# Turning the gated product in 32x32 blocks and through DRAM in place of TensorE transposes

## The chip, the cores and the metric

One core of a Trainium2 chip runs the whole program. The metric is the device time of one execution in microseconds, taken as the median of several runs.

## What is computed

Two transformer-like blocks follow each other on 256 rows of 1024 values in float32. The first has four feed-forward networks (FFNs) of width 2816 around a convolution module and a latent attention; the second has two, with a mixer between them and with modulation vectors that a product of a condition vector with a large matrix gives. An FFN is what the change touches:

```python
def swiglu_ffn(h, w1, w3, w2):
    return (jax.nn.silu(h @ w1) * (h @ w3)) @ w2

def first_block(...):
    for i in range(DEPTH):
        h = h + FFN_RES_WEIGHT * swiglu_ffn(rmsnorm(h, ffn_norm1[i]), ffn1_w1[i], ffn1_w3[i], ffn1_w2[i])
        m = rmsnorm(h, mix_norm[i])
        ...
        h = h + FFN_RES_WEIGHT * swiglu_ffn(rmsnorm(h, ffn_norm2[i]), ffn2_w1[i], ffn2_w3[i], ffn2_w2[i])

# second block, around the mixer, with shift, scale and gate from mod = silu(c) @ w_mod + b_mod
x = x + 0.5 * g1 * swiglu(modulate(rmsnorm_2(x, norm_ffn1), sh1, sc1), w_ffn1_in, w_ffn1_out)
...
x = x + 0.5 * g3 * swiglu(modulate(rmsnorm_2(x, norm_ffn2), sh3, sc3), w_ffn2_in, w_ffn2_out)
```

## The kernel before

Each float32 operand is split into a high part in fp32r and the rest, also in fp32r; `mm3` (L108) makes a product of three matrix products (high by high, high by low, low by high). `split` (L82, L83) has ScalarE write the high part and VectorE the low one. Weights come in units of 1 MB (128 rows of 2048 values): SP loads one into one of four `raw` buffers (L63), and `piece` splits it in four parts of 512 columns into `whi` and `wlo`. Of these there are 16 for W1 and W3, two steps' worth, and 8 for W2, two steps' worth as well.

The 256 rows are two row tiles, t = 0 and 1. An FFN goes through its width in eleven steps j of 256 columns (`NF = 11`). In a step, `load(j)` brings two units of W1 and W3 and one of W2; `gu(j, t)` makes the 24 products of `cols` (h with W1 beside W3, into a PSUM bank with the tag `wk`) and the gate: ScalarE writes the silu `sg` (L340), VectorE the gated product `gg` (L342), 128 rows by 256. For the product with W2 it must lie the other way round, so `turn(j, t)` has TensorE transpose it in two blocks of 128x128 against a unit matrix (L106), into a `wk` bank, and splits the result into `gh` and `gl`. `down(j, t)` makes 12 products of it with W2 and adds them up in the two `acc` banks of its row tile. Of a normal step the program has gu(j, 0), gu(j, 1), then down(j - 1, 0), turn(j, 0), down(j - 1, 1), turn(j, 1). The last step does gu(10, 0), down(9, 0), turn(10, 0) and half of cols(10, 1) before down(10, 0), so that row tile 0 is done early.

A planner orders the instructions of each engine ahead of time by what it thinks is ready, in the order of the program where several are. While `self.pinned` is set, TensorE's instructions keep the program's order (L99 to L106). In the FFNs that is so for steps 0 and 1 only. Each engine then works through its list in order, and an instruction that waits holds back those behind it. SP issues all transfers before the change.

In f0 to f4 a step with an even j, from 2 on, also makes a group of modulation values (`mid`, `mod_group`): four steps in f0, f1 and f2, three in f3 and f4, 18 in all. It loads two units, sums them with VectorE in `macc` (L987, L991), splits the sum, makes two products, loads a row of bias into `mrow` (L1001), adds it (L1002) and stores the row to DRAM (L1015). f5 has none.

In the convolution, the kernel already takes data through DRAM: `ship` (L570, L577) writes 128 partitions of 2 runs of 636 bytes and reads them back in four transfers of 32 partitions of 8 runs of 624 bytes, on SP's queue.

Of the kernel before, what the change touches and what calls it, by code (L numbers as in the profile page):

```python
# [10 lines left out]
F32 = mybir.dt.float32  # L11
F32R = mybir.dt.float32r
# [7 lines left out]
P = 128  # L20
# [11 lines left out]
class Build:  # L32
# [284 lines left out]

    def ffn(self, w, finish, after, mid=None, slow=False, begun=None):
        nc, tc = self.nc, self.tc
        with tc.tile_pool(name=f"ffn{self.n}", bufs=1) as fp:  # L320
            self.fp = fp
            acc = [[self.bank(tag="acc") for _ in range(2)] for _ in range(2)]
            g, w2 = {}, {}

            u = {}

            def up(j):
                u[j] = [self.unit(w[3 * j + i]) for i in range(2)]

            def down_in(j):  # L330
                w2[j] = self.unit(w[3 * j + 2], pool=fp)

            def load(j):
                up(j)
                down_in(j)

            def gate(j, t, ps):
                sc = 1.0 if self.rs[t] is None else self.rs[t][:, :1]
                sg = self.t([P, 256], tag="sg", bufs=2, pool=fp)
                nc.scalar.activation(sg, ps[:, :256], AF.Silu, scale=sc)  # L340
                g[j, t] = self.t([P, 256], tag="gg", bufs=3, pool=fp)
                nc.vector.scalar_tensor_tensor(  # L342
                    out=g[j, t], in0=ps[:, 256:], scalar=sc, in1=sg, op0=ALU.mult, op1=ALU.mult
                )

            def gu(j, t):
                gate(j, t, self.cols(t, u[j], 512))

            def turn(j, t):
                hi = self.t([P, 2, P], F32R, tag=f"gh{t}", bufs=2, pool=fp)  # L350
                lo = self.t([P, 2, P], F32R, tag=f"gl{t}", bufs=2, pool=fp)
                self.transposed(g[j, t], 2, hi, lo)
                g[j, t] = hi, lo

            def down(j, t):
                self.rows(acc[t], g[j, t], w2[j], j == 0, j == NF - 1)

            if begun:
                u[0] = begun[0]
                for t in range(2):  # L360
                    gate(0, t, begun[1][t])
                with self.in_turn():
                    up(1)
                turn(0, 0)
                gu(1, 0)
                down_in(0)
                turn(0, 1)
                gu(1, 1)
                turn(1, 0)
                down_in(1)  # L370
            else:
                load(0)
                load(1)
                gu(0, 0)
                gu(1, 0)
                self.flush()
                turn(0, 0)
                gu(0, 1)
                turn(1, 0)
                gu(1, 1)  # L380
                turn(0, 1)
            down(0, 0)
            turn(1, 1)
            down(0, 1)
            self.pinned = False
            for j in range(2, NF - 1):
                load(j)
                gu(j, 0)
                gu(j, 1)
                if mid:  # L390
                    mid(j)
                for t in range(2):
                    down(j - 1, t)
                    turn(j, t)
            j = NF - 1
            load(j)
            gu(j, 0)
            down(j - 1, 0)
            turn(j, 0)
            ps = self.cols(1, u[j], 512, ks=range(4))  # L400
            down(j, 0)
            finish(0, acc[0])
            post = after(0)
            gate(j, 1, self.cols(1, u[j], 512, ps, range(4, 8)))
            down(j - 1, 1)
            turn(j, 1)
            if not slow:
                post()
            down(j, 1)
            finish(1, acc[1])  # L410
            self.pending.append(after(1))
            if slow:
                post()

    def out_rows(self, x, units, finish, after, mid=None):


        acc, done, post = {}, [0, 0], []

        def step(order):  # L420
            for c in order:
                if c in "pm":
                    (post[0] if c == "p" else mid)()
                    continue
                t = int(c)
                if t not in acc:
                    acc[t] = [self.bank(tag="acc") for _ in range(2)]
                i = done[t]
                z = tuple(v[:, 2 * i : 2 * i + 2] for v in x[t])
                self.rows(acc[t], z, units[i], i == 0, i == 3)  # L430
                done[t] += 1
                if i == 3:
                    finish(t, acc[t])
                    (self.pending if t else post).append(after(t))

        return step
# [539 lines left out]
    def mod_group(self, i):  # L976

        nc, a = self.nc, self.a
        part, which, cols = i // 6, i % 6 // 2, slice(i % 2 * 512, i % 2 * 512 + 512)
        acc = self.t([P, 512], tag="macc", pool=self.fp)  # L980
        for u in range(2):
            r = self.raw(a["wmod"][2 * i + u])
            for k in range(4):
                w = r[:, k * 512 : k * 512 + 512]
                s = self.cact[:, 4 * u + k : 4 * u + k + 1]
                if u == k == 0:
                    nc.vector.tensor_scalar(  # L987
                        out=acc, in0=w, scalar1=s, scalar2=None, op0=ALU.mult
                    )
                else:  # L990
                    nc.vector.scalar_tensor_tensor(  # L991
                        out=acc, in0=w, scalar=s, in1=acc, op0=ALU.mult, op1=ALU.add
                    )
        hi = self.t([P, 512], F32R, tag="mhi", pool=self.fp)
        lo = self.t([P, 512], F32R, tag="mlo", pool=self.fp)
        self.split(hi, lo, acc)
        ps = self.bank()
        self.matmul(ps, self.onesr, hi, start=True, stop=False)
        self.matmul(ps, self.onesr, lo, start=False, stop=True)
        row = self.t([1, 512], tag="mrow", pool=self.fp)  # L1000
        nc.sync.dma_start(out=row, in_=a["b_mod_2"][0:1, i * 512 : i * 512 + 512])  # L1001
        nc.vector.tensor_add(row, ps[:1, :], row)  # L1002
        if which == 1:
            name = ("norm_ffn1_2", "norm_mix_2", "norm_ffn2_2")[part]
            grow = self.t([P, 512], tag="junk")[:1]
            nc.sync.dma_start(out=grow, in_=a[name][0:1, cols])
            nc.vector.scalar_tensor_tensor(
                out=row, in0=row, scalar=1.0, in1=grow,
                op0=ALU.add, op1=ALU.mult,
            )  # L1010
        elif which == 2:
            nc.vector.tensor_scalar(
                out=row, in0=row, scalar1=0.5, scalar2=None, op0=ALU.mult
            )
        nc.sync.dma_start(out=self.mods[i], in_=row)  # L1015
# [553 lines left out]
```

## Time and profile before

| | us |
|---|---|
| median of 3 runs | 1547.34 |
| lowest, highest | 1544.97, 1547.45 |
| the profiled execution's own time | 1546.88 |
| its span in the profile | 1545.1 |
| TensorE busy | 1517.2 |
| VectorE busy | 1093.9 |
| ScalarE busy | 831.2 |
| GpSimd busy | 36.0 |

The span reaches from the first to the last recorded instruction, and the profiled execution's own time is 1.8 us longer. An engine is busy while one of its instructions runs; matrix products overlap, so that TensorE's busy time is no measure of its speed. The DMA engines' share is that of the 16 engines' time in which packets were under way.

### The profile page before, as it was taken

Reading aid. Unit: us, or ns where it says so; the run is one execution under the profiler, and the core shown is the slowest. Engines: PE = TensorE matmul, PEld = TensorE weight load, DVE = VectorE, ACT = ScalarE, POOL = GpSimd, SP = SyncE. Lnnn points to the kernel's source line nnn. Section 1 sums busy time; section 2 is a strip of 40 time slices with the busy share of each in tenths; the row PEclk is TensorE's granted clock in tenths of the full one; section 3 lists DMA queues with packets and bytes.
Section 4 is the critical chain, followed back from the end, with each engine's and each line's share of the span. In section 5 each row is a group of like instructions: output and inputs, shape, how many; then the busy total and the mean of one; then the engine's idle time right before and its main releaser. Section 6 shows DMA issues by size and latency. Waiting matters only on the chain.

```text
span 1545.1 us, 21226 instructions
## 1 busy us (share of the span) xinstructions
PE 1517.2 (98%) x7824; PEld 1240.3 (80%) x7824; DVE 1093.9 (71%) x2136; ACT 831.2 (54%) x1723; POOL 36.0 (2%) x52
## 2 busy tenths in 40 slices
PE   8999998999999999999999999999999999999998
PEld 6888887788888888888788888788887877888886
DVE  7977566487775877657579765788657886876552
ACT  7555463465554655446475554545545565665541
POOL 0000000000000000000000000100001100000000
PEclk9999999999999999999999999999999999999999
DMA  8886477377664576643358755387552443565530
GB/s 312 305 291 252 171 239 186 115 277 284 245 245 164 218 270 249 235 137 119 127 195 310 263 191 191 127 307 275 207 191 95 161 167 112 192 255 186 196 109 28
DMA packets 61580, 316.69 MB, mean 205 GB/s; under 512 B 9210, under 2 KB 19706, under 8 KB 25764
## 3 DMA queue, kind: packets, MB, share of 16 engines
q1 hardware_dynamic: 61476, 315.34, 57.4%
q8 instruction: 61, 1.00, 0.3%
q14 instruction: 43, 0.35, 0.1%
HBM read 312.93 MB, written 2.39 MB: 204 GB/s over the span
## 4 chain that ended last, share of the span: by engine, by line
PE 90%; DVE 4%; issue 2%; DMA 2%; ACT 1%; POOL 1%; SPq 0%; POOLq 0%; DVEq 0%; ACTq 0%
PE wk L103 51%; PE acc L103 35%; PE wk L106 4%; DVE wlo L83 1%; DMA raw<-in_pw_dram 1%; POOL sm L130 1%; DMA h<-in_x_dram 0%; DVE sm L1190 0%; DMA shift<-ut 0%; DVE y L259 0%; DVE h L1033 0%; DVE y L1032 0%; DMA shifted<-shift 0%; ACT pb L1202 0%; DVE pb L1243 0%
## 5 line engine op out<-in xcount | busy, mean ns | idle before, releaser
L83 DVE TENSOR_TENSOR wlo<-raw,whi 128x512 fp32r<-128x512 f32 x996 | 652.3, 684 | 62.9 <-ACT whi L82 60.8
L82 ACT CAST whi<-raw 128x512 fp32r<-128x512 f32 x996 | 587.7, 619 | 95.4 <-PE acc L103 24.3
L103 PE MATMUL wk<-whi,xh 128*128 128x512 f32 x1120 | 443.8, 396 | 0.5
L103 PE MATMUL wk<-whi,xl 128*128 128x512 f32 x1120 | 437.8, 391 | 0.0
L103 PE MATMUL wk<-wlo,xh 128*128 128x512 f32 x1120 | 437.7, 391 | 0.0
L103 PEld LDWEIGHTS wk<-whi,xl 128*128 128x128 f32 x1120 | 210.9, 188 | 45.0
L103 PEld LDWEIGHTS wk<-whi,xh 128*128 128x128 f32 x1120 | 211.1, 188 | 43.5 <-ACT xh L85 1.5
L103 PEld LDWEIGHTS wk<-wlo,xh 128*128 128x128 f32 x1120 | 211.1, 188 | 42.1
L103 PE MATMUL acc<-whi,gh 128*128 128x512 f32 x528 | 212.2, 402 | 0.9 <-ACT gh L82 0.9
L103 PE MATMUL acc<-whi,gl 128*128 128x512 f32 x528 | 207.3, 393 | 0.0
L103 PE MATMUL acc<-wlo,gh 128*128 128x512 f32 x528 | 206.7, 392 | 0.0
L340 ACT ACTIVATE sg<-wk,sm 128x256 f32<-128x256 f32 x88 | 41.7, 474 | 196.5 <-PE wk L103 195.1
L342 DVE SCALAR_TENSOR_TENSOR gg<-wk,sm,sg 128x256 f32<-128x256 f32 x88 | 42.3, 481 | 110.4 <-ACT sg L340 109.1
L103 PE MATMUL acc<-whi,xh 128*128 128x512 f32 (+2 forms) x304 | 117.9, 389 | 0.7 <-ACT xh L82 0.7
L103 PEld LDWEIGHTS acc<-whi,gl 128*128 128x128 f32 x528 | 99.1, 188 | 21.7
L103 PEld LDWEIGHTS acc<-whi,gh 128*128 128x128 f32 x528 | 99.3, 188 | 21.4 <-ACT gh L82 2.1
L103 PE MATMUL acc<-wlo,xh 128*128 128x512 f32 (+2 forms) x304 | 116.1, 382 | 0.0
L103 PE MATMUL acc<-whi,xl 128*128 128x512 f32 (+2 forms) x304 | 115.7, 382 | 0.0
L103 PEld LDWEIGHTS acc<-wlo,gh 128*128 128x128 f32 x528 | 99.4, 188 | 19.9
L82 ACT CAST gh<-wk 128x256 fp32r<-128x256 f32 x132 | 48.8, 370 | 121.4 <-PE wk L106 121.3
L83 DVE TENSOR_TENSOR gl<-wk,gh 128x256 fp32r<-128x256 f32 x132 | 55.4, 419 | 64.4 <-ACT gh L82 64.3
L991 DVE SCALAR_TENSOR_TENSOR macc<-raw,cact,macc 128x512 f32<-128x512 f32 x126 | 94.4, 749 | 2.8
(278 smaller groups left out, 1162.1 us busy)
## 6 DMA issues: line engine op xcount, KB each, us to landing
raw<-in_f_dram SPq DMA_DIRECT2D x196, 1024.0 KB
raw<-in_wmod_dram SPq DMA_DIRECT2D x36, 1024.0 KB
raw<-in_win_dram SPq DMA_DIRECT2D x16, 1024.0 KB
raw<-in_pw_dram SPq DMA_DIRECT2D x12, 1024.0 KB
shifted<-shift SPq DMA_DIRECT2D x32, 156.0 KB
raw<-in_wo_dram SPq DMA_DIRECT2D x4, 1024.0 KB
raw<-in_wbr_dram SPq DMA_DIRECT2D x4, 1024.0 KB
raw<-in_wout_dram SPq DMA_DIRECT2D x4, 1024.0 KB
```

The lines of the kernel that those rows point to most:

```text
L82: i = nc.scalar.copy(hi, src)
L83: j = nc.vector.tensor_tensor(out=lo, in0=src, in1=hi.bitcast(F32), op=ALU.subtract)
L103: return self.pin(self.nc.tensor.matmul(*args, **kw))
L106: return self.pin(self.nc.tensor.transpose(out, src, ident))
L130: self.nc.gpsimd.tensor_tensor(out=r, in0=v, in1=self.mhalf[:, :1].to_broadcast([P, w]), op=ALU.pow)
L340: nc.scalar.activation(sg, ps[:, :256], AF.Silu, scale=sc)
L342: nc.vector.scalar_tensor_tensor(out=g[j, t], in0=ps[:, 256:], scalar=sc, in1=sg, op0=ALU.mult, op1=ALU.mult)
L991: nc.vector.scalar_tensor_tensor(out=acc, in0=w, scalar=s, in1=acc, op0=ALU.mult, op1=ALU.add)
```

## The change

In steps 1 to 9 the gated product is turned without TensorE. VectorE transposes each block of 32x32 within its place (`blocks`), both row tiles into one tile `gb`. Four transfers that GpSimd issues (`move`), one for every 32 partitions, write the blocks to DRAM, each block's row of 32 values (128 bytes) to where it belongs, 512 such runs per transfer. One more (`back`) reads the turned product into `gt`, 128 partitions of four runs of 512 bytes, and ScalarE and VectorE split it from there. Each step has its own place in DRAM. Steps 0 and 10 keep the transposes on TensorE.

In the program's order, `move(j)` stands behind gu(j, 1) and `back(j)` behind down(j - 1, 1). The last step is now pinned to the program's order. Two things change to make room: `gg` has two buffers in place of three, and the row of bias is loaded into row 0 of `macc`, once that is split, and not into a tile of its own.

```diff
     def ffn(self, w, finish, after, mid=None, slow=False, begun=None):
         nc, tc = self.nc, self.tc
-        with tc.tile_pool(name=f"ffn{self.n}", bufs=1) as fp:
+        with ExitStack() as ctx:
+            name = f"ffn{self.n}"
+            fp = ctx.enter_context(tc.tile_pool(name=name, bufs=1))
+            dram = ctx.enter_context(
+                tc.tile_pool(name=name + "d", bufs=1, space=bass.MemoryType.DRAM)
+            )
...
-                g[j, t] = self.t([P, 256], tag="gg", bufs=3, pool=fp)
+                g[j, t] = self.t([P, 256], tag="gg", bufs=2, pool=fp)
...
+            def parts(t):
+                return tuple(
+                    self.t([P, 2, P], F32R, tag=f"{n}{t}", bufs=2, pool=fp) for n in ("gh", "gl")
+                )
+
             def turn(j, t):
-                hi = self.t([P, 2, P], F32R, tag=f"gh{t}", bufs=2, pool=fp)
-                lo = self.t([P, 2, P], F32R, tag=f"gl{t}", bufs=2, pool=fp)
-                self.transposed(g[j, t], 2, hi, lo)
-                g[j, t] = hi, lo
+                pair = parts(t)
+                self.transposed(g[j, t], 2, *pair)
+                g[j, t] = pair
+
+            turned = {}
+
+            def blocks(j, t):
+
+                if t == 0:
+                    turned[j] = self.t([P, 2, 256], tag="gb", pool=fp)
+                nc.vector.transpose(turned[j][:, t], g[j, t])
+
+            def move(j):
+
+                d = dram.tile([2, 2, P, P], F32, name=f"{name}_{j}")
+                to = d.rearrange("t k (c f) (a s) -> a f (t k c) s", f=32, s=32)
+                for a in range(4):
+                    nc.gpsimd.dma_start(
+                        out=to[a],
+                        in_=turned[j][32 * a : 32 * a + 32].rearrange("p t (b s) -> p (t b) s", s=32),
+                    )
+                turned[j] = d
+
+            def back(j):
+                r = self.t([P, 2, 2, P], tag="gt", pool=fp)
+                nc.gpsimd.dma_start(
+                    out=r.rearrange("p t k s -> p (t k) s"),
+                    in_=turned[j].rearrange("t k p s -> p (t k) s"),
+                )
+                for t in range(2):
+                    g[j, t] = parts(t)
+                    self.split(*g[j, t], r[:, t])
...
                 gu(1, 0)
+                blocks(1, 0)
                 down_in(0)
                 turn(0, 1)
                 gu(1, 1)
-                turn(1, 0)
+                blocks(1, 1)
                 down_in(1)
...
+            move(1)
             down(0, 0)
-            turn(1, 1)
             down(0, 1)
+            back(1)
             self.pinned = False
             for j in range(2, NF - 1):
                 load(j)
-                gu(j, 0)
-                gu(j, 1)
+                for t in range(2):
+                    gu(j, t)
+                    blocks(j, t)
+                move(j)
                 if mid:
                     mid(j)
                 for t in range(2):
                     down(j - 1, t)
-                    turn(j, t)
+                back(j)
+            self.pinned = True
             j = NF - 1
             load(j)
             gu(j, 0)
...
             if slow:
                 post()
+            self.pinned = False
...
-        row = self.t([1, 512], tag="mrow", pool=self.fp)
+        row = acc[:1]
```

## Rows read from the trace of the kernel before

**Rows 1.** The page's first part: busy us, share of the span and instructions
```profile
PE 1517.2 (98%) x7824; PEld 1240.3 (80%) x7824; DVE 1093.9 (71%) x2136; ACT 831.2 (54%) x1723; POOL 36.0 (2%) x52
```

**Rows 2.** The chain that ended last, shares by engine and by line
```profile
PE 90%; DVE 4%; issue 2%; DMA 2%; ACT 1%; POOL 1%; SPq 0%; POOLq 0%; DVEq 0%; ACTq 0%
PE wk L103 51%; PE acc L103 35%; PE wk L106 4%; DVE wlo L83 1%; DMA raw<-in_pw_dram 1%; POOL sm L130 1%; DMA h<-in_x_dram 0%; DVE sm L1190 0%; DMA shift<-ut 0%; DVE y L259 0%; DVE h L1033 0%; DVE y L1032 0%; DMA shifted<-shift 0%; ACT pb L1202 0%; DVE pb L1243 0%
```

**Rows 3.** Windows of one f5 step and of two f1 steps: engines' busy us
```profile
core 0: us, PE busy (x) PEld busy (x) DVE busy (x) ACT busy (x) POOL busy (x), PEclk, DMA share, GB/s
1382.07:1398.97 16.90, 16.90 (x77) 13.85 (x77) 9.54 (x17) 8.69 (x16) 0.00 (x0) 1.00 0.54 194
357.08:391.21 34.13, 34.13 (x156) 28.09 (x155) 26.45 (x45) 17.92 (x33) 0.00 (x0) 1.00 0.71 254
```

**Rows 4.** The chain in order of time, f0 and f5: start us, us, what
```profile
161.19 10.93 PE wk L103 x48
...
178.04 5.49 PE wk L103 x24
...
1409.89 2.77 PE acc L103 x12
1412.88 2.77 PE acc L103 x12
1415.87 10.92 PE wk L103 x48
```

**Rows 5.** TensorE's timeline, last step of f0: start us, us, instruction
```profile
183.36 0.39 PE L103 MATMUL acc<-whi,gh 128*128 128x512 f32 x1
```

**Rows 6.** Timeline of a step in f1 and one in f5
```profile
370.80 0.39 PE L103 MATMUL acc<-whi,gh 128*128 128x512 f32 x1
...
371.88 0.48 DVE L342 SCALAR_TENSOR_TENSOR gg<-wk,sm,sg 128x256 f32<-128x256 f32 x1
...
1392.83 0.40 PE L103 MATMUL acc<-whi,gh 128*128 128x512 f32 x1
...
1393.61 0.42 DVE L342 SCALAR_TENSOR_TENSOR gg<-wk,sg 128x256 f32<-128x256 f32 x1
...
1395.60 0.38 PE L106 MATMUL wk<-ident,gg 128*128 128x128 f32 x2
...
1396.02 0.37 ACT L82 CAST gh<-wk 128x256 fp32r<-128x256 f32 x1 [2.10 <-PE wk L106]
```

**Rows 7.** VectorE's groups by line and form: busy us, mean ns, idle before
```profile
L83 DVE TENSOR_TENSOR wlo<-raw,whi 128x512 fp32r<-128x512 f32 x980 | 645.7, 687 | 61.4 <-ACT whi L82 59.3 <-DMA raw<-in_f_dram 0.5
...
L83 DVE TENSOR_TENSOR gl<-wk,gh 128x256 fp32r<-128x256 f32 x132 | 55.4, 419 | 64.4 <-ACT gh L82 64.3
...
L987 DVE TENSOR_SCALAR macc<-raw,cact 128x512 f32<-128x512 f32 x18 | 8.7, 484 | 8.6 <-DMA raw<-in_wmod_dram 8.5
...
L1280 DVE TENSOR_SCALAR pb<-pb,sm 128x256 f32<-128x256 f32 x16 | 4.6, 349 | 0.1
```

**Rows 8.** The convolution's transfers on SP: issue ns min/median/max, first and last start
```profile
L577 SPq DMA_DIRECT2D shifted<-shift x32: 303/448/1233, 216.5 to 271.0; - x32
L570 SPq DMA_DIRECT2D shift<-ut x8: 360/377/397, 213.9 to 264.8; - x8
```

**Rows 9.** SP's timeline in the convolution: one write and its reads
```profile
213.89 0.38 SPq L570 DMA_DIRECT2D shift<-ut  x1
216.50 1.83 SPq L577 DMA_DIRECT2D shifted<-shift  x4
```

**Rows 10.** The chain in order of time: waits for the convolution's transfers
```profile
254.44 5.67 DMA shift<-ut
262.30 3.84 DMA shifted<-shift
```

**Rows 11.** DMA view of 217 to 220 us: packets, and the queue's share
```profile
DMA packets 957, 0.57 MB, mean 189 GB/s; under 512 B 48, under 2 KB 957, under 8 KB 957
...
q1 hardware_dynamic: 957, 0.57, 88.7%
```

**Rows 12.** What SP's queue waited for: us in total, times, longest us
```profile
SPq L63 <- DVE wlo L83: 770.1, 173, 21.1
```

More of the change, by code (lines that the diff above doesn't have):

```diff
@@ L375, in ffn @@
                 gu(1, 0)
+                blocks(1, 0)
                 self.flush()
@@ L378, in ffn @@
                 gu(0, 1)
-                turn(1, 0)
                 gu(1, 1)
+                blocks(1, 1)
                 turn(0, 1)
+            move(1)
             down(0, 0)
-            turn(1, 1)
             down(0, 1)
+            back(1)
             self.pinned = False
```

## The prediction

> **What bounds the kernel now.** I read the busy shares first. TensorE has work in 1517.2 of 1545.1 us; GpSimd has 52 instructions and is free [rows 1]. The chain that ended last says the same from its end: 90% is TensorE, 51% in the products with W1 and W3, 35% in the accumulation with W2, and 4% in the transposes by line 106 [rows 2]. So a shorter TensorE program is a shorter kernel wherever nothing else comes late. Two stretches show how much else there is: a step without a modulation group has VectorE busy 9.54 of 16.90 us and the transfers at 0.54 of the DMA engines' time; two steps with one group between them have 26.45 of 34.13 us and 0.71. TensorE is busy all the time in both [rows 3].
>
> The chain in order of time gives the step's parts. 48 products take 10.92 us, and 12 accumulations 2.77 us, but the next piece begins 1412.88 - 1409.89 = 2.99 us later: the two transposes of one turn stand between and take 0.22 us [rows 4]. They last 0.38 us by themselves, but overlap with their neighbours [rows 6].
>
> **What is removed.** The turns of steps 1 to 9, two row tiles each, in six FFNs: 108 turns of 0.22 us, 23.8 us of TensorE. All lie on the chain. The step becomes 16.90 - 0.44 = 16.46 us. Steps 0 and 10 keep theirs.
>
> **What is put in its place, and how long it takes.** The new path starts where cols(j, 1) ends and must be done when down(j, 0) begins. I add it up from that end:
> - Gate: in one step without a group the product is written at 1393.61 + 0.42 us, 1.20 us after the first accumulation started at 1392.83; in a step with one, 371.88 + 0.48 - 370.80 = 1.56 us [rows 6]. I take 1.4.
> - The transpose on VectorE isn't in the trace. Its shape, 128x256 in f32, costs 349 ns as a tensor-scalar and 419 ns with two operands [rows 7]: 0.35 to 0.42, and up to 0.69 more behind one weight piece. I take 0.5. The 108 of them add 45 us to VectorE; a pair of steps goes to about 28.1 of 33.2 us, which TensorE's own time covers. If that cover went, they would cost 0.4 us each.
> - Four transfers out of 512 runs of 128 bytes, then one back of 512 runs of 512 bytes, all issued by GpSimd. No row shows GpSimd issuing. Nearest is SP with 32 partitions of 8 runs: 0.30 us at the least, 0.45 in the median, 1.23 at the most [rows 8]. I keep 0.30 as the low end, and twice 1.23, for twice the runs, as the high one. Runs written out by a program are nearer the slow rows than the fast: I take 1.0 each, so 4.0 for the four.
> - Landing of the last of them: the convolution writes 159 KB and starts its read 216.50 - 213.89 - 0.38 = 2.2 us after issue [rows 9]; in a crowded place the wait was 5.67 us [rows 10]. I take 2.6, since weights are loaded beside it.
> - Issue of the transfer back 1.0, again 0.30 to 2.46. Its landing: 3.84 us where the convolution waited for its read [rows 10], 2.2 as in the write at best; I take 3.0.
> - The high part on ScalarE before the first accumulation: 0.37 us [rows 6], 0.6 with a hand-over.
>
> Sum: 1.4 + 0.5 + 4.0 + 2.6 + 1.0 + 3.0 + 0.6 = 13.1 us. All low ends give 7.8, all high ends about 25.6.
>
> The Trainium skill has a price of its own, in "DMA: Bandwidth & Descriptors", section "Anatomy of one DMA — SWDGE (gpsimd) path": some 2.0 us fixed for a GpSimd transfer plus its bytes at 436 GB/s, issue included, which would be an estimate of 2.15 us for the last one out and 2.6 us for the one back. No row here shows such a transfer. With it the path would be 1.4 + 0.5 + 3.0 + 2.15 + 2.6 + 0.6 = 10.3 us and the forecast that of the first rival below.
>
> **The time there is for it.** In a regular step, down(j - 1) and cols(j + 1) lie between: 5.54 + 10.92 = 16.46 us. 13.1 fits, with 3.4 to spare. At the last step it doesn't: step 10 does only cols(10, 0) before down(9, 0), and TensorE's order is now pinned there. In the first FFN cols(9) ends at 161.19 + 10.93 = 172.12 and the first accumulation of down(9, 0) starts at 183.36 [rows 4, 5]: 11.24 us, less two turns 10.8. So TensorE waits 13.1 - 10.8 = 2.3 us once in each FFN, 13.8 us in six. In f5, where nothing comes after, the same holds.
>
> **The other edits.** Two buffers for the product in place of three: the next write of a buffer is a step later, 16 us against a path that has read it after 2. The bias row now lies in row 0 of the modulation sum, so its load, on SP, waits until VectorE has split that sum, and the add on VectorE waits for the load. Behind it on SP stand the next weight loads, behind the add on VectorE the next weight pieces. A landing of 2.2 us, 18 times, is 40 us of delay in all; SP waits 770.1 us for VectorE to free weight buffers anyway [rows 12], and VectorE has some 5 us left in each pair of steps. I cost it at nothing; with that cover gone it is 40 us.
>
> The transfers add 2560 packets to a step. Where small ones ran alone, 957 packets took 88.7% of 16 engines for 3 us, 44 ns each [rows 11]; by bytes a 128-byte one would be 9 ns and a 512-byte one 36. A step gets 2.3 to 7.0 us of the DMA engines' time. The plain step goes from 9.1 to at most 16.1 of 16.46 us. The pair with a group goes from 24.2 to between 28.8 and 38.2 of 33.2: that can fail. I take the middle, 33.5, which just about fits, and cost it at nothing.
>
> **Sum.** 1546.88 us, the profiled execution's own time (span 1545.1 and 1.8 around it), less 23.8 plus 13.8, is 1536.9. The median of the three runs is 0.5 us above that execution, so 1537.
>
> **Rivals.**
> 1. All hidden: the path is under 10.8 us, as it is if an issue costs 0.5 us. Then 23.8 us are gained: 1523.5. For it, SP's median; against it, the runs per issue.
> 2. A little later than I think: between 14.25 and 15.3 us the six waits give back all but 3.1 us of the gain, or exceed it by no more: no change, 1544 to 1550.
> 3. Late in every step, the opposite sign. Place: the issue on GpSimd, one after another. At 1.9 us each the path is 17.6 us. Each FFN's last wait is 6.8 us, 41 in all; in the eight regular steps TensorE waits for 17.6 - 16.46 = 1.1 us at every second one (a wait gives the next path that much more room), 27 in all: 1546.9 - 23.8 + 41 + 27 = 1591. It decides from 15.3 us of path. The steps between aren't pinned, and the planner may put cols(j + 2, 0) ahead of down(j, 0) where it sees the lateness coming; that would take the 27 away, not the 41.
> 4. The transfers become the bound in the FFNs with groups: 38.2 against 33.2 us is 5 us a pair, 18 pairs, 90 us: 1627 with the forecast's own terms; at 35 ns a packet 2.2 a pair, 1577. For it: loads there already arrive at 0.71. Against: 44 ns is of packets of 624 bytes.
> 5. VectorE holds GpSimd's descriptor writing off. If GpSimd only got on in VectorE's gaps, its 5.0 us of issue would grow by 1 / (1 - 26.45 / 34.13) = 4.4 in a pair with a group: 22 us, a path of 30, some 13 late at every second step. With half of the 48 regular windows as such places, 24 x 13.6 + 6 x 19 less 23.8 is over 400 us; the time would be near 1960. Against it: the frequent pieces run at 687 ns for 512 elements with two operands, and only a form like the tensor-scalar of 484 ns, 18 in all, goes faster over the same 512 [rows 7]. The Trainium skill states this rule in "SBUF — State Buffer", section "Who interferes with whom", for VectorE's two-port modes; no run here shows it yet.
>
> **How the numbers follow.** Chances: the forecast (path 10.8 to 14.25, gain 3 to 24) 0.36; rival 1 0.11; rival 2 0.11; rival 3 0.25; rival 4 0.12; rival 5 0.05. A change under 0.2%, 3.1 us, can't be told from none here. So faster 0.47, same 0.11, slower 0.42. The predicted time is that of the forecast, whose own range is 1523 to 1544. The range of 8 in 10 reaches from 1520, just below rival 1, to 1612, where the path is 18.3 us: what is left out is the upper part of rivals 3 and 4, and rival 5.
>
> **What would show it.** Transposes of gg on line 106 fall from 264 to 48, and a step without waits is 16.46 us. Right: GpSimd's issues near 1.0 us, no wait of TensorE in the middle of an FFN, one of about 2 us before down(9, 0). Wrong: issues near 2 us with TensorE waiting for gh in the steps between (rival 3), a DMA share of 1.0 between weight loads and ScalarE waiting for raw (rival 4), issues that get longer where VectorE is busier (rival 5), or a TensorE wait behind the modulation row.

## The result, and the profile after

The changed kernel takes 1612.95 us in the median of four runs (1607.09 to 1615.57), the kernel before 1546.65 us (1544.97 to 1547.45). The ratio is 1.0426, with a 95% interval of 1.0414 to 1.0439: slower by 66 us, where the forecast was 1537 us and 10 us gained. The profiled execution took 1614.23 us, with a span of 1612.5.

The page of the kernel after, its first part, the GpSimd queue of its DMA part, and the chain that ended last by engine and by line:

```profile
PE 1517.0 (94%) x7608; PEld 1227.3 (76%) x7608; DVE 1113.0 (69%) x2244; ACT 814.1 (50%) x1723; POOL 217.5 (13%) x322
...
q0 software_dynamic: 11232, 28.33, 6.0%
...
PE 52%; DMA 23%; DVE 11%; ACT 5%; issue 4%; POOL 4%; SPq 0%; POOLq 0%; ACTq 0%; DVEq 0%
PE acc L103 26%; PE wk L103 25%; DMA gt<-ffn 12%; DMA ffn<-gb 8%; DVE wlo L83 5%; POOL ffn L377 3%; ACT whi L82 2%; PE wk L106 2%; ACT gh L82 1%; DMA raw<-in_f_dram 1%; DVE gg L347 1%; DVE gb L370 1%; DMA raw<-in_wmod_dram 1%; POOL sm L130 0%; DMA raw<-in_pw_dram 0%
```

TensorE has its 216 instructions less than in [rows 1], but the chain, 90% TensorE in [rows 2], now lies on TensorE for half of the time. For the rest it goes through the transfers and the engines that hand the product on.

The windows of one step of f5, and of the 7 us after one wait in f1, halved (the columns of [rows 3]):

```profile
1462.83:1479.25 16.42, 16.42 (x73) 13.51 (x72) 11.27 (x21) 9.30 (x19) 3.35 (x5) 1.00 0.65 224
399.00:402.50 3.50, 3.40 (x9) 2.73 (x10) 3.35 (x7) 3.50 (x9) 0.00 (x0) 0.58 0.33 132
402.50:406.00 3.50, 3.50 (x17) 2.87 (x16) 3.50 (x7) 3.44 (x7) 0.68 (x2) 1.00 0.54 169
```

In f5 the change did what it should: a step of 16.42 us without a wait, against 16.90 in [rows 3]. Behind a wait of 3.06 us, which ends at 399.10 us in f1, the granted clock is 0.58 on average over the next 3.5 us (a mix of 1.2 and 2.4 GHz), and 9 matmuls start there. In the 3.5 us after, at 1.00, 15 start (the row's 17 counts two that had begun before). A long wait is paid again behind it. TensorE's timeline has the start of that step's products, the end of the wait, and the end of the next one:

```profile
385.00 0.39 PE L103 MATMUL wk<-whi,xh 128*128 128x512 f32 x1
...
399.10 0.80 PE L103 MATMUL acc<-whi,gh 128*128 128x512 f32 x1 [3.06 <-ACT gh L82]
...
419.04 0.51 PE L103 MATMUL acc<-whi,gh 128*128 128x512 f32 x1 [1.51 <-ACT gh L82]
```

What TensorE waited for (us in all, times, longest):

```profile
PE acc L103 <- ACT gh L82: 67.8, 37, 6.7
```

Its timeline at the last step of f0, where [rows 5] had a start without a wait:

```profile
207.15 0.80 PE L103 MATMUL acc<-whi,gh 128*128 128x512 f32 x1 [6.73 <-ACT gh L82]
```

There are 37 such waits, of 67.8 us. Ahead of down(9, 0), from one start to the next, 7.1, 5.2, 3.8, 2.5, 3.6 and 1.2 us pass in f0 to f5; without a wait it is 0.23, so 22 us are lost there. Nearly all of the rest, 45 us, lies in the regular steps of f0 to f4, those with a modulation group and those between. 1546.9 - 23.8 + 67.8 = 1590.9 us; the other 23 us up to 1614.2 fit matmuls at the lower clock. The kernel "gate first" below has the same instructions and hardly a wait: against it, TensorE is idle for 66 us more and busy for 28.7 us more (1517.0 against 1488.3 us). The accumulations with gh and gl alone are busy for 641.8 us here and for 619.8 us there.

GpSimd's issues of the writes, by their line (ns min/median/max, first and last start), which answer to SP's in [rows 8]:

```profile
L377 POOL DMA_DIRECT2D ffn<-gb x216: 648/649/1179, 39.2 to 1581.5; - x108
```

The issues of the reads, in GpSimd's groups (busy us, mean ns, idle time before them):

```profile
L385 POOL DMA_DIRECT2D gt<-ffn x54 | 41.5, 769 | 273.1 <-DMA ffn<-gb 172.9 <-ACT whi L82 70.9 <-ACT sg L345 23.6
```

The transposes, in VectorE's groups by form, beside [rows 7]:

```profile
L370 DVE STREAM_TRANSPOSE gb<-gg 128x256 f32<-128x256 f32 x108 | 47.3, 438 | 12.6 <-DMA ffn<-gb 11.5
```

The transfers' median us from issue to landing, where [rows 9, 10] had 2.2 to 5.67:

```profile
ffn<-gb POOLq DMA_DIRECT2D x216, 64.0 KB, 5.1
gt<-ffn POOLq DMA_DIRECT2D x54, 256.0 KB, 3.5
```

An issue of a write takes 0.65 us where 1.0 was forecast, and a transpose 0.44 us; the landing of the write takes twice as long as was forecast. The timelines of ScalarE, VectorE and GpSimd in one step of f5 (the lines of the product alone):

```profile
1464.22 0.37 ACT L345 ACTIVATE sg<-wk 128x256 f32<-128x256 f32 x1
...
1465.28 0.42 DVE L347 SCALAR_TENSOR_TENSOR gg<-wk,sg 128x256 f32<-128x256 f32 x1
1466.21 0.44 DVE L370 STREAM_TRANSPOSE gb<-gg 128x256 f32<-128x256 f32 x1
...
1466.94 2.59 POOL L377 DMA_DIRECT2D ffn<-gb  x4 [8.42 <-DVE gb L370]
1473.52 0.77 POOL L385 DMA_DIRECT2D gt<-ffn  x1 [3.99 <-DMA ffn<-gb]
...
1476.96 0.71 ACT L82 CAST gh<-gt 128x256 fp32r<-128x256 f32 x2 [0.29 <-DMA gt<-ffn]
```

The same in f1, beside a modulation group:

```profile
398.65 0.71 ACT L82 CAST gh<-gt 128x256 fp32r<-128x256 f32 x2 [7.53 <-DMA gt<-ffn]
399.26 0.62 ACT L82 CAST whi<-raw 128x512 fp32r<-128x512 f32 x1
399.79 0.61 ACT L82 CAST mhi<-macc 128x512 fp32r<-128x512 f32 x1
400.30 1.66 ACT L82 CAST whi<-raw 128x512 fp32r<-128x512 f32 x3
401.87 0.47 ACT L345 ACTIVATE sg<-wk,sm 128x256 f32<-128x256 f32 x1
...
402.93 0.48 DVE L347 SCALAR_TENSOR_TENSOR gg<-wk,sm,sg 128x256 f32<-128x256 f32 x1
...
403.93 0.44 DVE L370 STREAM_TRANSPOSE gb<-gg 128x256 f32<-128x256 f32 x1
...
405.32 2.59 POOL L377 DMA_DIRECT2D ffn<-gb  x4 [11.86 <-DVE wlo L83]
...
415.20 0.77 POOL L385 DMA_DIRECT2D gt<-ffn  x1 [7.29 <-DMA ffn<-gb]
...
418.58 0.71 ACT L82 CAST gh<-gt 128x256 fp32r<-128x256 f32 x2 [4.26 <-DMA gt<-ffn]
```

This is a loop. ScalarE stands 7.53 us before a split of a product that hasn't landed (398.65). The silu of the next step's second row tile is behind it on the same queue: the products of the step run from 385.00 us for 10.92, as in [rows 4], and are done at 395.92. ScalarE then does the split and five pieces, and the silu starts at 401.87. The next transfer starts as late, so the next split waits again at 418.58. One turn of the loop is 418.58 - 398.65 = 19.93 us, against 16.42 us that TensorE needs for the step.

### The profile page after: what moved, and what is told of

The parts are those of the page before. It is cut to its first block, busy times and chain, and to the rows that moved or that the text cites. A ratio compares the mean times of both kernels' runs of the same rounds, so it can differ in the third digit from the quotient of the medians.

```text
span 1612.5 us, 21564 instructions
## 1 busy us (share of the span) xinstructions
PE 1517.0 (94%) x7608; PEld 1227.3 (76%) x7608; DVE 1113.0 (69%) x2244; ACT 814.1 (50%) x1723; POOL 217.5 (13%) x322
## 3 DMA queue, kind: packets, MB, share of 16 engines
q0 software_dynamic: 11232, 28.33, 6.0%
## 4 chain that ended last, share of the span: by engine, by line
PE 52%; DMA 23%; DVE 11%; ACT 5%; issue 4%; POOL 4%; SPq 0%; POOLq 0%; ACTq 0%; DVEq 0%
PE acc L103 26%; PE wk L103 25%; DMA gt<-ffn 12%; DMA ffn<-gb 8%; DVE wlo L83 5%; POOL ffn L377 3%; ACT whi L82 2%; PE wk L106 2%; ACT gh L82 1%; DMA raw<-in_f_dram 1%; DVE gg L347 1%; DVE gb L370 1%; DMA raw<-in_wmod_dram 1%; POOL sm L130 0%; DMA raw<-in_pw_dram 0%
## 5 line engine op out<-in xcount | busy, mean ns | idle before, releaser
L83 DVE TENSOR_TENSOR wlo<-raw,whi 128x512 fp32r<-128x512 f32 x996 | 636.4, 680 | 54.2 <-ACT whi L82 51.6
L82 ACT CAST whi<-raw 128x512 fp32r<-128x512 f32 x996 | 574.9, 617 | 150.8 <-PE acc L103 74.5
L103 PE MATMUL wk<-whi,xh 128*128 128x512 f32 x1120 | 438.5, 391 | 0.8 <-ACT xh L82 0.3
L103 PE MATMUL acc<-whi,gh 128*128 128x512 f32 x528 | 217.1, 411 | 67.9 <-ACT gh L82 67.8
L377 POOL DMA_DIRECT2D ffn<-gb x216 | 141.4, 661 | 577.4 <-DVE gb L370 452.4
L103 PE MATMUL acc<-whi,gl 128*128 128x512 f32 x528 | 212.2, 402 | 2.5 <-DVE gl L83 2.5
L103 PE MATMUL acc<-wlo,gh 128*128 128x512 f32 x528 | 212.5, 402 | 0.0
L103 PEld LDWEIGHTS acc<-whi,gh 128*128 128x128 f32 x528 | 102.8, 195 | 104.6 <-ACT gh L82 84.9
L83 DVE TENSOR_TENSOR gl<-gt,gh 128x256 fp32r<-128x256 f32 x108 | 41.0, 421 | 102.6 <-ACT gh L82 102.6
L82 ACT CAST gh<-gt 128x256 fp32r<-128x256 f32 x108 | 38.4, 403 | 138.2 <-DMA gt<-ffn 138.2
```

The lines of the kernel that those rows point to most:

```text
L82: i = nc.scalar.copy(hi, src)
L83: j = nc.vector.tensor_tensor(out=lo, in0=src, in1=hi.bitcast(F32), op=ALU.subtract)
L103: return self.pin(self.nc.tensor.matmul(*args, **kw))
L377: nc.gpsimd.dma_start(out=to[a], in_=turned[j][32 * a : 32 * a + 32].rearrange("p t (b s) -> p (t b) s", s=32),)
```

## The experiments

The runs before beside which these stood had medians of 1545 to 1546 us. Letters in an expectation are explained in it; the A and B of "Two steps" are those of "No group loads": landings too late for the window, and ScalarE's order, which passes lateness on.

**No transfers.** The five transfers of a step are left out; the split reads the blocks that VectorE has turned, which aren't the turned product. All other edits stay.

```diff
 def move(j):
-    d = dram.tile([2, 2, P, P], F32, name=f"{name}_{j}")
...
-    turned[j] = d
+    pass
 def back(j):
-    r = self.t([P, 2, 2, P], tag="gt", pool=fp)
...
-        self.split(*g[j, t], r[:, t])
+        self.split(*g[j, t], turned[j][:, t].rearrange("p (k s) -> p k s", k=2))
```

> Leaves the five transfers of each step out: the split reads the 32x32-turned tile where it lies, so blocks are not moved between partitions. VectorE's transposes, the buffers, the pinned last step and the bias row stay as in the changed kernel. Theory A (the round trip through DRAM lands too late; everything else is harmless): all waits for gh go, 1523 to 1526 us, the 23.8 us of the removed turns below before. Rival C (VectorE's added transposes, fewer buffers or the bias row hold TensorE): waits stay in steps with a modulation group, above 1560 us.

Measured: 1521.79 us, ratio 0.9842 (0.9828 to 0.9857). That is 24.2 us less than before, and the forecast for the 108 turns was 23.8; the transposes, two buffers in place of three, the pinned orders and the bias row cost nothing that shows. All of the loss, 91 us, hangs on the transfers; whether on their traffic or on waiting for them, the next run tells.

**Dead transfers.** The kernel before, with its turns on TensorE, and beside them the transposes and five transfers of steps 2 to 9, whose data nobody reads (`back` has no split here), and the bias row.

```diff
 for t in range(2):
     gu(j, t)
+    blocks(j, t)
+move(j)
 for t in range(2):
     down(j - 1, t)
     turn(j, t)
+back(j)
```

> The kernel before with TensorE's turns kept, and beside them VectorE's transposes, the four transfers out and the one back in steps 2 to 9, whose result nobody reads; two-buffer rules as before, the bias row as after. Theory A (only being waited for costs): 1545 to 1551 us. Rival D (the 2560 small packets a step slow the weight loads themselves until TensorE runs dry): 1565 us or more, with ScalarE waiting for raw.

Measured: 1546.68 us, ratio 1.0004 (0.9995 to 1.0013). The packets cost nothing where nobody waits for them. They landed as slowly as in the changed kernel, 5.0 us out and 4.1 us back in the median; so the slow landing isn't made by the loop.

**Long runs.** The same, the writes as one run of 2048 bytes a partition.

```diff
-to = d.rearrange("t k (c f) (a s) -> a f (t k c) s", f=32, s=32)
+to = d.rearrange("t k (h q) s -> (t k) h (q s)", q=4)
...
-        in_=turned[j][32 * a : 32 * a + 32].rearrange("p t (b s) -> p (t b) s", s=32),
+        in_=turned[j][32 * a : 32 * a + 32].rearrange("p t s -> p (t s)"),
```

> The kernel before with the dead transfers, the writes to DRAM as one run of 2048 bytes a partition in place of sixteen of 128 bytes. If the landing of the write (5.0 us in the middle there) is the price of its 512 short runs, it falls under 3.5 us and the issue of 0.65 us gets shorter; if it is a fixed latency of a GpSimd transfer beside the weight loads, it stays at 4.5 to 5 us. The time of the kernel stays 1546 us either way.

Measured, in one execution: 1547.97 us; the issue falls from 656 to 506 ns on average, the landing from 5.0 to 4.6 us. Short runs are a small part of the landing. The trace of the changed kernel shows what goes with a larger part. From 1512 us, in step 5 of f5, weights are loaded beside the transfers; from 1561, in step 8, no longer. The queues and the transfers in the 16 us from 1512 us, then in the 12 us from 1561 us:

```profile
q1 hardware_dynamic: 432, 3.15, 55.9%
q0 software_dynamic: 208, 0.52, 9.7%
...
ffn<-gb POOLq DMA_DIRECT2D x4, 64.0 KB, 4.4
gt<-ffn POOLq DMA_DIRECT2D x1, 256.0 KB, 3.7
```

```profile
q0 software_dynamic: 208, 0.52, 21.8%
...
ffn<-gb POOLq DMA_DIRECT2D x4, 64.0 KB, 2.3
gt<-ffn POOLq DMA_DIRECT2D x1, 256.0 KB, 3.4
```

With nothing beside it a write lands 2.3 us after the start of its issue, in the median of the four; beside the weight loads it takes 4.4. Why it does is not shown.

**No group loads.** The 36 loads of modulation weights are left out; the groups multiply other data.

```diff
-r = self.raw(a["wmod"][2 * i + u])
...
-w = r[:, k * 512 : k * 512 + 512]
+w = self.h[u][:, k % 2 * 512 : k % 2 * 512 + 512]
```

> The changed kernel with the 36 loads of modulation weights left out; the groups' sums read the resident h, so VectorE and ScalarE do the same work on wrong numbers. Theory A (the landings are stretched by the groups' loads on the same 16 DMA engines): transfers land within some 4.4 and 3.4 us as in the FFN without groups, no waits in the steps, only the six last ones of 1 to 4 us: 1535 to 1546 us. Rival B (ScalarE's fixed order closes a loop, whatever the loads): steps stay near 18 to 20 us in part, 1560 us or more.

Measured: 1578.08 us, ratio 1.021 (1.0193 to 1.0227). In f1 up to 510 us the transfer back lands in 3.3 us in the median, not 4.4, and the gaps in its steps are nearly gone; over all FFNs six regular waits of 0.5 to 2.7 us and three shorter ones are left. It is the read that changes: in steps 2 to 8 of f0 to f4 it takes over 4 us from the end of its issue to its landing in 2 of 35 steps, against 15 of 35 with the group loads, while the waits for the write are nearly the same (5.3 against 5.5 us in the median). The waits ahead of down(9, 0) stay; these are those of f0 and f1:

```profile
190.32 0.79 PE L103 MATMUL acc<-whi,gh 128*128 128x512 f32 x1 [6.24 <-ACT gh L82]
...
496.99 0.79 PE L103 MATMUL acc<-whi,gh 128*128 128x512 f32 x1 [6.39 <-ACT gh L82]
```

The time is on the side of 1560 us or more, the gaps in the steps are on the other. So there are two losses. The steps lie at the edge, and the group loads push them over; the last step's window is too short with them or without. Leaving the loads out also frees `raw` buffers and SP's queue, and no run tells these from the traffic.

**Step 9 on TensorE**, in the changed kernel, then also without the group loads.

```diff
 load(j)
+last = j == NF - 2
 for t in range(2):
     gu(j, t)
-    blocks(j, t)
-move(j)
+    if not last:
+        blocks(j, t)
+if not last:
+    move(j)
...
 for t in range(2):
     down(j - 1, t)
-back(j)
+    if last:
+        turn(j, t)
+if not last:
+    back(j)
```

> The changed kernel with step 9 turned on TensorE again (steps 1 to 8 stay with the transfers). Theory: the six waits ahead of down(9,0) in the last step (7.1, 4.9, 3.8, 2.5, 3.6 and 1.2 us, 23 us in all) go, with some 8 us of matmuls at the lower clock behind them, and twelve turns of 0.22 us come back: 1613 - 23 - 8 + 3 = 1585 us (1575 to 1595); the gaps inside the steps stay as they are. Rival: the last step's wait is only where a delay of the whole FFN shows (late weights, say), and it turns up elsewhere: 1600 us or more.

> As the one before, and without the 36 loads of modulation weights (the groups multiply by other data that is in SBUF). Theory: the two losses add up and are all there is. From the kernel without any transfer (1521.8 us) by twelve turns (2.6 us) and the 10.5 us of gaps that the run without group loads showed inside its steps, with some clock: 1530 to 1546 us. Rival: a loss of each FFN that belongs to neither: 1560 us or more.

Measured: 1587.81 us (ratio 1.0273, 1.0247 to 1.03) and 1543.12 us (0.9983, 0.9965 to 1.0). Both lie in the ranges of the two losses, the second in the upper part of its own. Apart, step 9 on TensorE and no group loads give 25 and 35 us, together 70: ten more than their sum, as where one lateness feeds the next.

**Two steps between gate and down.** down(j - 2) in step j, the W2 load a step later; step 10 does down(8), down(9) and down(10).

```diff
 def load(j):
     up(j)
-    down_in(j)
+    down_in(j - 1)
...
 for t in range(2):
-    down(j - 1, t)
+    down(j - 2, t)
 back(j)
...
```

> The changed kernel with the accumulation two steps behind instead of one: down(j - 2) stands in step j, the W2 unit is loaded a step later, and in the last step down(8, 0), down(8, 1) stand ahead of down(9, 0). The time for the round trip grows from 16.46 to 32.9 us, at the end from 10.8 to about 16.5. Theories A and B both: waits go, 1523 to 1530 us, below before. Rival C: no better than 1590 us. If the loop through ScalarE's queue has no slack to lose, some waits stay in f0: 1535 us.

Measured: 1607.5 us, ratio 1.0391 (1.0348 to 1.0434). That is far from the expected 1523 to 1530 us: a window of twice the length gained 5 us, hardly more than the scatter (1597 to 1614 us, and 1607 to 1616 for the changed kernel). In f1 TensorE has one gap in the regular steps from the third on, of 0.6 us, but three in the last one, of 4.7, 2.0 and 5.0 us (11.7 us idle; the next expectation's 13.4 is too much). ScalarE's timeline in that stretch of f1:

```profile
444.27 0.71 ACT L82 CAST gh<-gt 128x256 fp32r<-128x256 f32 x2 [8.13 <-DMA gt<-ffn]
444.89 2.18 ACT L82 CAST whi<-raw 128x512 fp32r<-128x512 f32 x4
446.98 0.47 ACT L345 ACTIVATE sg<-wk,sm 128x256 f32<-128x256 f32 x1
447.34 2.69 ACT L82 CAST whi<-raw 128x512 fp32r<-128x512 f32 x5
449.94 0.46 ACT L345 ACTIVATE sg<-wk,sm 128x256 f32<-128x256 f32 x1
...
465.51 0.71 ACT L82 CAST gh<-gt 128x256 fp32r<-128x256 f32 x2 [3.47 <-DMA gt<-ffn]
...
483.78 0.71 ACT L82 CAST gh<-gt 128x256 fp32r<-128x256 f32 x2 [8.18 <-DMA gt<-ffn]
```

The silu at 446.98 us is that of a step's second row tile. In TensorE's timeline the last of its products starts at 433.01 us, so it has stood behind the split, which waits until 444.27 us. The silu at 449.94 is that of the next step's first row tile; the one of its second row tile, whose last product starts at 449.81, stands behind the next split and starts only at 468.74. The splits come 21.2 and 18.3 us apart here, the steps of TensorE 16.8 on average. The loop goes on where TensorE waits for nothing, and the longer window only saves the lateness up for the end of the FFN.

**Gate first.** The kernel of two steps, with the split of a landed product behind the silu and the transposes of the next step's second row tile.

```diff
 move(j)
+land(j - 1)
...
 def back(j):
...
-    for t in range(2):
-        g[j, t] = parts(t)
-        self.split(*g[j, t], r[:, t])
+    turned[j] = r
+def land(j):
+    with tc.issue_after(self.sg.ins), tc.issue_after(self.gg.ins):
+        for t in range(2):
+            g[j, t] = parts(t)
+            self.split(*g[j, t], turned[j][:, t])
```

(`sg` and `gg` keep the last silu and the last transpose.)

> The kernel with down two steps behind, with one thing added: on ScalarE and VectorE the split of a landed product comes behind the silu and the block transposes of the next step's second row tile, where it stood ahead of them. Theory (feedback by ScalarE's order: a late landing delays the next gate, so the next transfer starts late, and the lateness adds up over the eight steps to the last one): the last step's gaps in f1, 13.4 us before, fall below 5 us, and the time to 1540 to 1575 us. Rival (landing alone sets it, the order does nothing): as the kernel two steps behind, 1595 us or more.

Measured: 1522.62 us, ratio 0.9852 (0.9832 to 0.9872): 90 us less than the changed kernel, 23 less than before, and more than was expected. ScalarE's timeline in f1:

```profile
451.90 0.47 ACT L345 ACTIVATE sg<-wk,sm 128x256 f32<-128x256 f32 x1 [3.71 <-PE wk L103]
...
457.58 0.47 ACT L345 ACTIVATE sg<-wk,sm 128x256 f32<-128x256 f32 x1
457.95 0.70 ACT L82 CAST gh<-gt 128x256 fp32r<-128x256 f32 x2
```

A window of 141.5 us there:

```profile
346.50:488.00 141.50, 141.50 (x630) 117.16 (x629) 107.61 (x192) 74.16 (x149) 24.81 (x37) 1.00 0.77 268
```

TensorE's group of first accumulations, from the page, idle time last:

```profile
L103 PE MATMUL acc<-whi,gh 128*128 128x512 f32 x528 | 207.2, 392 | 1.4 <-ACT gh L82 1.4
```

Here the silus start when their products are made, and TensorE is busy without a gap at full clock. Over the whole run its idle time for gh is 1.4 us; the engines' busy time, from the page:

```profile
PE 1488.3 (98%) x7608; PEld 1218.4 (80%) x7608; DVE 1116.8 (74%) x2244; ACT 814.2 (54%) x1723; POOL 219.5 (14%) x322
```

The transfers land no sooner: 4.9 us out and 4.2 us back in the median of the whole run. The time is within 1 us of the kernel without any transfers, so landings of this length cost nothing here.

**Gate first, and step 9 on TensorE.**

```diff
 load(j)
+last = j == NF - 2
 for t in range(2):
     gu(j, t)
-    blocks(j, t)
+    if not last:
+        blocks(j, t)
...
     down(j - 2, t)
+    if last:
+        turn(j, t)
...
```

> The one before, and step 9 turned on TensorE. Theory: no landing is waited for any more, so the time is that of the kernel without any transfer and twelve turns more: 1521.8 + 2.6 = 1524 us, 1520 to 1532. Rival: the modulation groups' loads or late weights keep part of the loss however early the product lands: 1545 us or more.

Measured: 1527.41 us, ratio 0.9882 (0.9863 to 0.99). In the range, but 5 us slower than the one before: there was no wait left to remove, and twelve turns, 2.6 us, came back. The rest is open.

**Gate first, one step.** The order alone, in the changed kernel.

```diff
 move(j)
+land(j - 1)
...
 for t in range(2):
     down(j - 1, t)
```

> The changed kernel, down one step behind as it is, with the new order alone: the split of a landed product behind the silu and the block transposes of the next step's second row tile. Theory: the lateness no longer adds up, but each down(j-1) now has to wait for the silu that runs after the last cols matmul before it (about 0.2 us of landing in PSUM, 0.46 us of silu, 0.36 us of split, some 1.2 us in all), in every step of every FFN, f5 too where the changed kernel had no gap: 1522 + 48 x 1.2 + the last steps = 1585 us or somewhat more (1575 to 1610). Both halves, order and two steps, are then needed. Rival: the order alone is what matters: 1550 us or less.

Measured: 1579.68 us, ratio 1.0234 (1.0209 to 1.026). The total fits, one reason doesn't: f5 has no wait of 1.2 us. Two starts of down there, from TensorE's timeline:

```profile
1425.34 0.50 PE L103 MATMUL acc<-whi,gh 128*128 128x512 f32 x1
...
1441.92 0.50 PE L103 MATMUL acc<-whi,gh 128*128 128x512 f32 x1
```

A step is 16.58 us, 0.16 more than without the order: ScalarE starts the silu of the second row tile at 1441.19 us while products go on to 1441.67 and later, so those are already of another step: the planner has filled the wait with them. The loss is in f0 to f4, where 33.7 of the 35.7 us lie that TensorE still waits for gh. They have two causes. In the last steps, and in 6 of the 21 late regular steps, the split waits for a landing. In the other 15, with 13.0 of 18.7 us, the product has landed 0.6 to 7.7 us before and stands behind the silu: there the new order itself is what TensorE waits for, as the expectation had it.

**Control: before, two steps.** The kernel before, turns on TensorE, with the same two steps.

```diff
 for t in range(2):
-    down(j - 1, t)
+    down(j - 2, t)
     turn(j, t)
...
```

> A control: the kernel before, all turns on TensorE, with down two steps behind and the W2 load a step later, no transfers. Theory: what the kernel with both new orders gained over before (23 us) is the 108 turns alone, and two steps between gate and down are worth nothing where no landing is waited for: 1546 us (1540 to 1553). Rival: a good part of the gain is the longer distance itself, and this kernel has it too: 1535 us or less.

Measured: 1544.89 us, ratio 0.9986 (0.9974 to 0.9999). The distance by itself is worth next to nothing; the 23 us of the kernel with gate first are the turns.

Against the changed kernel, then, the distance alone gives 5 us, the order alone 33, both 90. Neither does it alone: without the order the lateness adds up past two steps, and without the distance TensorE meets late landings, and splits that stand behind the silu.

## Why the prediction was wrong

The step that failed is the path: "13.1 fits, with 3.4 to spare". Its terms, from the end of cols(j, 1) to the first accumulation, in the two steps shown above (in f5 from 1462.83 us, in f1 from 395.92 to 419.04; a landing is counted from the end of its issue to the start of what waits for it):

| term | forecast | f5 | f1 |
|---|---|---|---|
| gate, to the product written | 1.4 | 2.9 | 7.5 |
| transpose, with its wait | 0.5 | 0.9 | 1.0 |
| four issues, with the wait ahead | 4.0 | 2.9 | 3.5 |
| landing of the write | 2.6 | 4.0 | 7.3 |
| issue back | 1.0 | 0.8 | 0.8 |
| landing of the read | 3.0 | 2.7 | 2.6 |
| high part | 0.6 | 0.4 | 0.5 |
| sum | 13.1 | 14.5 | 23.1 |

By the same count the path has a median of 14.2 us in steps 2 to 7 of f5. In steps 2 to 8 of f0 to f4 it is 19.8 us, and over the 16.46 us of the window in 29 of 35; the gate has a median of 5.2 us there, the landing of the write one of 5.5.

- **The landing of the write** was mis-sized: 2.6 us from a transfer on SP's queue; 4.0 and 7.3 here. In steps 8 and 9 of f5, where no weights are loaded, it is 2.2 and 2.1 us: the weights beside it were in the forecast with 0.4 us. The estimate by the Trainium skill ("DMA: Bandwidth & Descriptors", section "Anatomy of one DMA — SWDGE (gpsimd) path") was 2.15 us for the write, with the issue in it. The trace agrees only where nothing is loaded beside it (2.3 us from issue to landing); over the whole run the median is 5.1 us, and the rows decide. For the read the estimate was 2.6 us, against 3.5 in the median and 3.4 with nothing beside it.
- **The landing of the read** was mis-sized too, though the two steps of the table don't show it: it took 4.2 to 7.2 us in 15 of the 35 steps, and 5.2 us ahead of the wait that ends at 399.10 us.
- **The gate** was taken from steps of before, where no split of a landed product stands ahead of it on ScalarE. Here one does, and in f1 6.0 of its 7.5 us pass before the silu starts: ScalarE stands before the split until 398.65 us and then has the split, four pieces of weights and one of the modulation sum ahead. So 1.4 us was no constant but depended on how late the last landing was. The prediction worked out a wait as giving "the next path that much more room"; with this order it starts the next path later too. This missing feedback is what turned steps over their window into steps late one after another; two steps with and without the new order, 85 us apart, show it.
- **The last step** was in the forecast with 2.3 us a time. It took 0.9 to 6.9 us, 22 us and not 13.8, and some clock behind it.
- **The clock behind a wait** was in no term. The waits themselves leave 23 us unexplained; they point to it, and so do the 28.7 us that TensorE is busy longer than with hardly a wait. No run took it away by itself.
- **Right** were the 23.8 us of the turns (24.2 by the kernel without transfers), a step of 16.42 us for 16.46, and no cost for the bias row, the buffers and VectorE's 47.3 us.
- **Right by luck**: no cost of the packets as such. The forecast had 2560 a step and 2.3 to 7.0 us of the DMA engines' time, and its middle, 33.5 us, was over the 33.2 us that it was to fit in. The trace counts 11232 / 54 = 208 a step, and 6.0% of 1612.5 us / 54 = 1.8 us. (All high ends of the path come to 25.1 us, not 25.6; nothing hangs on it.)

Of the rivals, the third had the place where it shows, late in regular steps, and its 1591 us are 22 off; but it came there by GpSimd's issues at 1.9 us, and they took 0.65. The time of 1627 us in the fourth is nearer still, by luck: packets that nobody waits for cost nothing (the dead transfers), and TensorE waited for gh, not for weights. The second, no change, would have needed about f5's path everywhere. The first (all hidden, 1523.5) came true only with the split behind the gate and two steps to land. The fifth falls with the issues: 166 of the 216 ran while VectorE was busy throughout, with a median of 649 ns, and 21 while it was nearly idle, with one of 664. The rule in the Trainium skill ("SBUF — State Buffer", section "Who interferes with whom") is for VectorE's two-port modes; the trace shows no hold-up here.

## What to carry to other kernels

When work moves from a compute engine to a transfer, look at what stands behind the first instruction that waits for its landing, on the same in-order queue: if the next transfer's source is made there, lateness is passed on, and a longer window alone did not cure it here. Put what starts the next transfer ahead of what waits for the last one, then give the landing a step more; measure the two apart and together. A variant without the transfers and one with transfers that nobody reads tell in two runs whether the loss is the wait or the traffic.

## What the hardware showed unexpectedly

- A transfer of 64 KB out of 512 runs of 128 bytes took GpSimd 649 ns to issue in the median, over 700 in 8 of 216, and landed 2.2 to 7.5 us after the start of its issue, 5.1 in the median. With runs of 2048 bytes the issue fell from 656 to 506 ns on average and the landing from 5.0 to 4.6 us.
- With no weight loads beside them, such transfers landed in 2.3 us in the median; with them, in steps of the same FFN, in 4.4.
- 9984 more packets, and 96 transposes on VectorE, cost nothing measurable while no engine waited for them (1.0004).
- A wait of 3.06 us was followed by 3.5 us at a mean granted clock of 0.58, in which 9 matmuls started for 15 at 1.00.
